# A matmul in two levels of fast products: GpSimd's additions tied to VectorE's order, and a new order of the work

## The chip, the cores and the metric

The kernel runs on one core of one Trainium2 chip. The metric is the device time of one execution in microseconds; before the change it is 1467.53 us, the median of three executions (1467.13, 1467.53 and 1470.08).

## The reference

```python
def setup_inputs():
    B, S, D = 8, 2048, 2048
    return {
        "x": np.random.randn(B, S, D).astype(np.float32),
        "w": np.random.randn(D, D).astype(np.float32),
    }

def reference(x, w):
    cs = np.cumsum(x, axis=1)
    diff = cs - np.concatenate([np.zeros((cs.shape[0], 1, cs.shape[2]), dtype=np.float32), cs[:, :-1, :]], axis=1)
    return np.matmul(diff, w).astype(np.float32)
```

The difference of a running sum is the input again, so what is computed is the product x w of a 16384 x 2048 and a 2048 x 2048 matrix.

## The kernel before

The 16384 rows are 128 tiles of 128 rows. The first 4 are multiplied plainly, since the blocks of w arrive meanwhile. The other 124 go in 31 **groups** (periods 0 to 30 in the code) of four tiles g, h, k and l. All matmuls are f16 with sums in f32, 128 x 128 by 128 x 512; four of them on one part of the contraction are a **quarter**.

A group computes a 2 x 2 block scheme of fast multiplication (tiles g, h against k, l, and the two halves of the columns), with additions in place of multiplications. Six of its products, P1, P2, P5, P3, P4 and P7, are themselves split once more into seven quarters (class `Seven`, L452; P1.0 to P1.6 on TensorE); the seventh, P6, is done whole for g and for h (P6g.0.0 and so on, L527). That makes 50 quarters, or 200 matmuls, in a group.

The names that the text uses, for a product such as P5:

- P5.s1 to P5.s4 (L463): VectorE additions of 128 x 512 f16 pieces of x, the left inputs of quarters 1, 2, 4 and 5.
- in5.Q1 (and Q4; L385): a VectorE addition of 128 x 2048 f16 pieces of w, the right input of quarter 1, made into the one buffer `flow` that all products share, so each waits until the quarter that last read it is done.
- P5.first, P5.out2 and P5.out4: ScalarE copies of the sum so far from one PSUM bank to another or to SBUF (`lent`); P5.middle: a VectorE addition that takes P5.out2 into another bank.
- S1g, S1h, S2h, S4g: VectorE additions of whole halves of tiles, 128 x 1024 f16, the inputs of the outer scheme.
- keep C11g.0, C11h+P2.0, C12g.1, C21h+P7.1: the results of the outer scheme in SBUF, f32, copied by ScalarE or added from PSUM by VectorE, 128 x 512 each.
- Twelve additions of two f32 128 x 512 pieces in SBUF are GpSimd's in each group: P2.last, P3.last, P7.last and P4.last (a `lent` copy onto a result), and C12g+C21, C12h+C21, C22g+C21 and C22h+C21, two each.

x arrives as f32 in three stages of a buffer F (`load`, L129, on SyncE's queue), is cast to f16 by ScalarE in place (`narrow`, L144), checked for its range by ScalarE (`weigh`, L148), and transposed by DMA into the tiles of x (`turn`, L160, on the same queue), which gives the stage back. turn7.0 fills half of the group's eighth tile (tiles 4 to 7 of a group's numbers are those of the next group). Results go out from the same queue (`put`, L506).

The plain part ends with copies out.1.3.1 and the like (half, tile, piece) of PSUM banks by ScalarE; their banks are those that P1 and P2 of group 0 use. ScalarE's casts narrow2.0 and narrow3.1 belong there too: they are for group 0's tiles.

What sets the order: every operation is first recorded with a label and its engine (`record`, L98), and at the end `emit` (L104) sorts all of them by the number that a table gives the label, plus 100000 for each period. Tables stand there for periods 0, 1, 2, 28, 29 and 30, and one (`None`) for the 25 steady groups, periods 3 to 27. `after` (L86) chains each operation to the one before it on its own engine, so each engine issues in the order of the numbers. Between engines only data decides: an operation waits for what it reads, and for those that still use what it writes.

Of the kernel before, what the change touches and what calls it, by code (L numbers as in the profile page):

```python
# [10 lines left out]
def kernel(  # L11
# [41 lines left out]
    B11, T1, B12, T2, B21, T3s, B22, T4 = (  # L53
        [fours[:, k, i // 2, i % 2] for k in range(KH)] for i in range(8)
    )
# [48 lines left out]
    def emit(places):  # L104
        def when(op):
            at, label = op[:2]
            own = places[at] if at in places else places[None]
            return at * PERIOD + own[label]

        for _, _, engine, ask in sorted(ops, key=when) if places else ops:  # L110
            after(engine, ask)
        ops.clear()

# [575 lines left out]
    def judge():  # L689
# [42 lines left out]
            'numbers': -648116, 'first x.1.0': -635524, 'first x.2.3': -593898,  # L732
            'first x.0.1': -583215, 'first x.0.3': -573021, 'cast w.0.1': -565802,
            'first x.0.2': -513040, 'first x.1.1': -509724, 'numbers turned': -509328,
# [517 lines left out]
```

## Time and profile before

| | |
|---|---|
| median of three executions | 1467.53 us |
| the profiled execution | 1465.45 us, of which the span is 1463.4 |
| TensorE busy | 1426.9 us, 97% of the span |
| VectorE, ScalarE, GpSimd busy | 1319.0, 1050.7, 531.5 us |
| GpSimd's additions | 372, mean 1445 ns |
| granted clock of TensorE, mean | 0.997 |

TensorE's busy time is the floor for this order of matmuls, so the question at each place is what TensorE waits for. VectorE is busy for 90% of the span and feeds TensorE, ScalarE and GpSimd; GpSimd is idle for two thirds of it. A line of the timeline gives the start, the time, the engine, the line of the code, the operation, out<-in, the count and, in brackets, the idle time before it and what ended that. The additions that `tensor` records are all on L116, copies and casts L119, quarters L440 and L533. Group 0 starts at about 72 us, group 3 at 213.5 and group 28 at 1317.5.

### The profile page before, as it was taken

How to read it: one execution, taken by the hardware profiler on the slowest of the kernel's cores; microseconds unless marked ns; L12 is line 12 of the kernel's file. 1: busy time of each engine (PE TensorE's matmuls, PEld its weight loads, DVE VectorE, ACT ScalarE, POOL GpSimd, SP SyncE). 2: the span in 40 equal slices, each digit the busy share in tenths (PEclk: the TensorE clock that was granted, in tenths of full speed). 3: DMA queues.
4: the chain of work that ended last, by engine and by line, in shares of the span. 5: the costliest groups of instructions: out<-in, count | busy, mean ns of one | idle time of the engine just before them, and what ended most of it. 6: DMA issues, size and time to landing. Idle time of an engine off the chain costs nothing. (4 is left out here: it accounts for less than half of the span.)

```text
span 1463.4 us, 20495 instructions
## 1 busy us (share of the span) xinstructions
PE 1426.9 (97%) x6543; PEld 631.4 (43%) x6543; DVE 1319.0 (90%) x2107; ACT 1050.7 (72%) x1716; POOL 531.5 (36%) x376
## 2 busy tenths in 40 slices
PE   8989999999999999999999999999999999999997
PEld 4434344444444444444444444444444444444443
DVE  2889889999999989999999999999999999999998
ACT  5877867777777777777777777777777677777663
POOL 0004432344433344423344423344423444423444
PEclk9999999999999999999999999999999999999999
DMA  9998778888787898888888888888788888888873
GB/s 365 345 245 225 202 222 240 250 230 237 231 255 234 239 232 241 231 238 248 244 236 241 231 240 249 252 228 246 223 251 248 240 235 233 224 251 239 259 213 120
DMA packets 343790, 351.62 MB, mean 240 GB/s; under 512 B 270976, under 2 KB 270976, under 8 KB 343680
## 3 DMA queue, kind: packets, MB, share of 16 engines
q1 hardware_dynamic: 343680, 350.29, 84.1%
q8 instruction: 52, 0.85, 0.2%
q14 instruction: 58, 0.48, 0.1%
HBM read 150.99 MB, written 134.22 MB: 195 GB/s over the span
## 5 line engine op out<-in xcount | busy, mean ns | idle before, releaser
L116 POOL TENSOR_TENSOR arena<-arena 128x512 f32<-128x512 f32 x372 | 531.3, 1445 | 926.7 <-DVE arena L116 728.2
L119 ACT COPY arena<-b 128x512 f32<-128x512 f32 x729 | 411.5, 590 | 267.9 <-PE b L440 197.0
L440 PE MATMUL b<-W,x 128*128 128x512 f16 x2108 | 526.6, 380 | 0.9 <-ACT b L119 0.4
L440 PEld LDWEIGHTS <-x 128*128 128x128 f16 x3224 | 313.0, 98 | 399.1 <-issue 20.8
L116 DVE TENSOR_TENSOR arena<-W 128x2048 f16<-128x2048 f16 (+1 forms) x287 | 359.9, 1255 | 45.0 <-PE b L440 44.6
L440 PE MATMUL b<-W,arena 128*128 128x512 f16 x1364 | 340.2, 379 | 9.4 <-ACT b L119 6.9
L440 PEld LDWEIGHTS <-arena 128*128 128x128 f16 x1984 | 192.5, 98 | 254.5 <-DVE arena L116 22.1
L440 PE MATMUL b<-arena,x 128*128 128x512 f16 x1116 | 286.0, 380 | 6.7 <-ACT arena L119 6.3
L119 ACT CAST F<-F 128x1024 f16<-128x1024 f32 x248 | 257.2, 1050 | 41.4 <-DMA F<-in_x_dram 40.5
L116 DVE TENSOR_TENSOR arena<-arena,b 128x512 f32<-128x512 f32 x372 | 250.9, 679 | 14.8 <-PE b L440 9.6
L153 ACT ACTIVATE F<-F 128x1024 f16<-128x1024 f16 x248 | 263.1, 1061 | 1.1
L533 PE MATMUL b<-W,x 128*128 128x512 f16 x992 | 240.5, 379 | 4.1 <-DVE x L116 2.9
L116 DVE TENSOR_TENSOR x<-x,x 128x1024 f16<-128x1024 f16 (+1 forms) x372 | 222.9, 607 | 12.2 <-PE b L440 3.3
L119 ACT COPY b<-b 128x512 f32<-128x512 f32 x186 | 107.8, 580 | 76.3 <-DVE arena L116 56.2
L440 PE MATMUL b<-arena 128*128 128x512 f16 x620 | 159.1, 379 | 2.6 <-DVE arena L116 2.2
L116 DVE TENSOR_TENSOR b<-b,arena 128x512 f32<-128x512 f32 x217 | 150.2, 693 | 8.8 <-ACT arena L119 7.6
L533 PEld LDWEIGHTS <-x 128*128 128x128 f16 x992 | 94.7, 98 | 128.3 <-DVE x L116 17.8
L116 DVE TENSOR_TENSOR arena<-b,arena 128x512 f32<-128x512 f32 x155 | 106.1, 685 | 20.4 <-PE b L440 20.2
L116 DVE TENSOR_TENSOR arena<-x 128x512 f16<-128x512 f16 x124 | 73.3, 591 | 0.1
L116 DVE TENSOR_TENSOR arena<-x,x 128x512 f16<-128x512 f16 x124 | 62.4, 503 | 3.7 <-PE b L440 1.4
L116 DVE TENSOR_TENSOR x<-x 128x512 f16<-128x512 f16 x124 | 64.4, 519 | 0.9
L254 PE MATMUL b<-W,arena 128*128 128x512 f16 x240 | 54.8, 379 | 2.6 <-ACT W L119 2.4
(43 smaller groups left out, 304.0 us busy)
## 6 DMA issues: line engine op xcount, KB each, us to landing
F<-in_x_dram SPq DMA_DIRECT2D x248, 512.0 KB, 5.1
out_dram<-arena SPq DMA_DIRECT2D x240, 512.0 KB, 5.4
W<-in_w_dram SPq DMA_DIRECT2D x32, 512.0 KB, 9.5
out_dram<-arena SPq DMA_DIRECT2D x32, 256.0 KB, 3.2
W<-in_x_dram SPq DMA_DIRECT2D x16, 256.0 KB, 6.5
x<-F SPq DMA_TRANSPOSE x248, 3.3
```

Source lines behind the costliest of these rows:

```text
L116: record(label, engine, lambda: on.tensor_tensor(dst, p, q, op))
L119: record(label, "act", lambda: nc.scalar.copy(to, p))
L153: return nc.scalar.activation(other, data, ABS, accum_out=m)
L254: said = nc.tensor.matmul(to[n], xP[:, r, ko, :], b[:, n, :], start=(ko == 0), stop=(ko == KO - 1))
L440: said = nc.tensor.matmul(to, a[:, ds(k * P, P)], b[:, k, :], start=(start and k == 0), stop=(k == 3), skip_group_check=True,)
L533: said = nc.tensor.matmul(to[n], half(t, 0)[:, k, :], T2[k][:, n, :], start=False, stop=(k == KH - 1), skip_group_check=True,)
```

## The change

`emit` now ties each GpSimd addition to the VectorE operation that was emitted last before it: the addition waits until that operation is done, whether or not it reads its result. And all seven tables are replaced. No operation is added, removed or given to another engine.

```diff
         for _, _, engine, ask in sorted(ops, key=when) if places else ops:
             after(engine, ask)
+            if engine == "pool" and "dve" in last:
+                in_turn(last["pool"], last["dve"])
         ops.clear()
+
+    def in_turn(later, first):
+        tc.add_manual_dep(
+            later.ins,
+            first.ins.name,
+            mybir.DependencyInfo(mybir.DependencyClass.Sync, mybir.DependencyReason.DATA),
+            reason="GpSimd after VectorE, in the order of places",
+        )
...
         None: {
...
-            'S2h': 13382, 'P6g.1.1': 13785, 'P5.s1': 13929, 'P2.4': 14251, 'P2.out4': 14372,
-            'P2.last': 15346, 'P2.5': 15487, 'C11g+P2.1': 15743, 'P2.6': 15807,
...
+            'C11h+P2.0': 18274, 'P6h.0.0': 20162, 'in5.Q1': 20364, 'P5.first': 20601,
+            'P2.last': 21182, 'P5.s2': 21300, 'load5.0': 23180, 'load4.0': 24591,
```

The lines of the code after the helper stand 10 lower than before (L116 is now L126, L119 is L129).

**VectorE in a steady group, around P2.last.** Rows give line, operation, out<-in with the buffers' numbers, and the shape. Before, from C11h+P2.1 to in5.Q1: C11h+P2.1, S1h, S2h, P5.s1, C11g+P2.1, C11h+P2.0, P5.s2, in5.Q1.

```order
L116 TENSOR_TENSOR arena_70<-arena_70,b7_81 128x512
L116 TENSOR_TENSOR x30_68<-x30_68,x31_69 128x1024
L116 TENSOR_TENSOR x10_64<-x30_68,x10_64 128x1024
L116 TENSOR_TENSOR arena_70<-x30_68 128x512
L116 TENSOR_TENSOR arena_70<-arena_70,b5_79 128x512
L116 TENSOR_TENSOR arena_70<-arena_70,b6_80 128x512
L116 TENSOR_TENSOR arena_70<-arena_70,x20_66 128x512
L116 TENSOR_TENSOR arena_70<-W_58 128x2048
```

And in the changed kernel, from S1h on: S1h, P5.s1, S2h, C11h+P2.0, in5.Q1, P5.s2, C11g+P2.1, S4g.

```order
L126 TENSOR_TENSOR x30_68<-x30_68,x31_69 128x1024
L126 TENSOR_TENSOR arena_70<-x30_68 128x512
L126 TENSOR_TENSOR x10_64<-x30_68,x10_64 128x1024
L126 TENSOR_TENSOR arena_70<-arena_70,b6_80 128x512
L126 TENSOR_TENSOR arena_70<-W_58 128x2048
L126 TENSOR_TENSOR arena_70<-arena_70,x20_66 128x512
L126 TENSOR_TENSOR arena_70<-arena_70,b5_79 128x512
L126 TENSOR_TENSOR x01_63<-x01_63,x00_62 128x1024
```

GpSimd's P2.last had its number behind P5.s1 and waited only for C11h+P2.1 and ScalarE's P2.out4; now it has its number behind in5.Q1 and waits for that too. C11h+P2.1 has moved up, C11g+P2.1 down behind P5.s2.

**VectorE at the seam of two steady groups.** Before, from C21g+P7.1: C21g+P7.1, P4.middle, C21h+P7.1, P4.s4, C21g+P4.0, in1.Q1 (of the next group), C21h+P7.0, P1.s2, C21g+P4.1, P1.s3.

```order
L116 TENSOR_TENSOR arena_70<-arena_70,b3_77 128x512
L116 TENSOR_TENSOR b7_81<-b5_79,arena_70 128x512
L116 TENSOR_TENSOR arena_70<-arena_70,b1_75 128x512
L116 TENSOR_TENSOR x21_67<-x21_67 128x512
L116 TENSOR_TENSOR arena_70<-arena_70,b6_80 128x512
L116 TENSOR_TENSOR arena_70<-W_58 128x2048
L116 TENSOR_TENSOR arena_70<-arena_70,b0_74 128x512
L116 TENSOR_TENSOR arena_70<-arena_70,x00_62 128x512
L116 TENSOR_TENSOR arena_70<-arena_70,b7_81 128x512
L116 TENSOR_TENSOR arena_70<-x00_62,x10_64 128x512
```

And in the changed kernel, from P4.middle: P4.middle, P4.s4, C21g+P4.0, C21h+P7.0, P1.s2, C21h+P7.1, in1.Q1, C21h+P4.0, C21g+P4.1, P1.s4, P1.s3.

```order
L126 TENSOR_TENSOR b7_81<-b5_79,arena_70 128x512
L126 TENSOR_TENSOR x21_67<-x21_67 128x512
L126 TENSOR_TENSOR arena_70<-arena_70,b6_80 128x512
L126 TENSOR_TENSOR arena_70<-arena_70,b0_74 128x512
L126 TENSOR_TENSOR arena_70<-arena_70,x00_62 128x512
L126 TENSOR_TENSOR arena_70<-arena_70,b1_75 128x512
L126 TENSOR_TENSOR arena_70<-W_58 128x2048
L126 TENSOR_TENSOR arena_70<-arena_70,b4_78 128x512
L126 TENSOR_TENSOR arena_70<-arena_70,b7_81 128x512
L126 TENSOR_TENSOR arena_70<-x00_62,arena_70 128x512
L126 TENSOR_TENSOR arena_70<-x00_62,x10_64 128x512
```

in1.Q1 has moved behind C21h+P7.0 and C21h+P7.1; C22h+C21.0 waits for C21h+P7.0, P7.last for C21h+P7.1 just ahead of in1.Q1, and C22h+C21.1 for P1.s4. On TensorE, P1.1, which needs in1.Q1, is now the fourth quarter of P1 to be issued (P1.0, P1.2, P1.3, P1.1) and P1.0 has moved up among the last quarters of the group before.

**ScalarE in the head, from the last copies of the plain part on.** Before: out.1.0.1, P1.out2, the two casts narrow2.0 and narrow3.1, P1.out4, out.1.3.0, out.1.3.1, out.1.2.0, P2.first.

```order
L119 COPY arena_70<-b1_75 128x512
L119 COPY arena_70<-b2_76 128x512
L119 CAST F_61<-F_61 128x1024 x2
L119 COPY arena_70<-b2_76 128x512
L119 COPY arena_70<-b6_80 128x512
L119 COPY arena_70<-b7_81 128x512
L119 COPY arena_70<-b4_78 128x512
L119 COPY b4_78<-b6_80 128x512
```

And in the changed kernel: out.1.2.1, P1.out2, out.1.2.0, out.1.3.0, P1.out4, narrow2.0, P2.first, out.1.3.1, narrow3.1.

```order
L129 COPY arena_70<-b5_79 128x512
L129 COPY arena_70<-b2_76 128x512
L129 COPY arena_70<-b4_78 128x512
L129 COPY arena_70<-b6_80 128x512
L129 COPY arena_70<-b2_76 128x512
L129 CAST F_61<-F_61 128x1024
L129 COPY b4_78<-b6_80 128x512
L129 COPY arena_70<-b7_81 128x512
L129 CAST F_61<-F_61 128x1024
```

P1.out4 and three copies of the plain part have moved ahead of the casts.

More of the change, by code (lines that the diff above doesn't have):

```diff
@@ L724 @@
         0: {
[7 rows of a table removed]
-            'numbers': -648116, 'first x.1.0': -635524, 'first x.2.3': -593898,
-            'first x.0.1': -583215, 'first x.0.3': -573021, 'cast w.0.1': -565802,
-            'first x.0.2': -513040, 'first x.1.1': -509724, 'numbers turned': -509328,
[157 rows of a table removed]
-        },
[47 rows of a table removed]
-        },
[46 rows of a table removed]
[7 rows of a table added]
+            'first x.0.0': -710913, 'cast w.0.0': -708588, 'numbers turned': -640017,
+            'eye': -620640, 'first x.0.1': -615478, 'first x.2.3': -611089,
[156 rows of a table added]
+        },
[47 rows of a table added]
+        },
[46 rows of a table added]
         },
         28: {
[44 rows of a table removed]
[44 rows of a table added]
         },
         29: {
[44 rows of a table removed]
[45 rows of a table added]
         },
         30: {
[42 rows of a table removed]
[43 rows of a table added]
         },
         None: {
[45 rows of a table removed]
[44 rows of a table added]
         },
```

856 rows, old and new, of the table places are left out of this document.

## The prediction

> **What bounds the kernel now.** I read the page first, then the busy time by stage, then what each engine waits for, then single groups of the timeline.
>
> ```profile
> span 1463.4 us, 20495 instructions
> PE 1426.9 (97%) x6543; PEld 631.4 (43%) x6543; DVE 1319.0 (90%) x2107; ACT 1050.7 (72%) x1716; POOL 531.5 (36%) x376
> L116 POOL TENSOR_TENSOR arena<-arena 128x512 f32<-128x512 f32 x372 | 531.3, 1445 | 926.7 <-DVE arena L116 728.2
> L116 DVE TENSOR_TENSOR arena<-x 128x512 f16<-128x512 f16 x124 | 73.3, 591 | 0.1
> ```
>
> TensorE is the bound at 97%; GpSimd has slack and waits mostly for VectorE already. The last row matters: VectorE's small f16 additions take 591 ns on average. By stage (start:end, length, then busy time of PE, PEld, DVE, ACT, POOL, clock, DMA share, GB/s), and for one good and one bad group:
>
> ```profile
> 0.00:213.50 213.50, 198.31 (x919) 87.42 (x919) 163.01 (x268) 157.47 (x239) 41.21 (x33) 0.98 0.89 269
> 213.50:1317.50 1104.00, 1093.45 (x5013) 485.02 (x5012) 1022.88 (x1631) 804.40 (x1330) 428.06 (x303) 1.00 0.85 239
> 1317.50:1463.40 145.90, 135.09 (x614) 58.94 (x612) 133.14 (x210) 88.83 (x148) 62.20 (x42) 0.99 0.72 207
> 350.40:393.92 43.52, 43.52 (x201) 19.41 (x200) 40.43 (x66) 32.12 (x53) 17.00 (x13) 1.00 0.87 249
> 525.85:571.00 45.15, 43.98 (x202) 19.32 (x201) 41.13 (x66) 32.08 (x53) 16.66 (x13) 1.00 0.89 234
> ```
>
> The second row is the 25 steady groups: 1104.00 / 25 = 44.16 us each. The fourth is one in which nothing goes wrong: 43.52. The fifth is group 10, which lost 1.6 us. So between a steady group and a clean one lie 25 x (44.16 - 43.52) = 16.0 us. The end of the chain of waits gives the floor:
>
> ```profile
> 1430.52 6.05 PE b L440 x28
> ...
> 1451.84 1.40 POOL arena L116
> ...
> 1458.48 0.69 DVE arena L116
> ```
>
> 28 matmuls in 6.05 us are 0.216 each; a quarter (4) is 0.865 and a group (200) 43.2. A clean group is thus within 0.32 us of the floor.
>
> The same place in a clean group (9) and in group 10, from the timeline:
>
> ```profile
> 500.53 1.56 POOL L116 TENSOR_TENSOR arena<-arena 128x512 f32<-128x512 f32 x1 [4.30 <-ACT arena L119]
> 500.54 0.42 DVE L116 TENSOR_TENSOR arena<-x 128x512 f16<-128x512 f16 x1
> 502.60 1.22 DVE L116 TENSOR_TENSOR arena<-W 128x2048 f16<-128x2048 f16 x1
> 503.12 1.03 PE L440 MATMUL b<-W,arena 128*128 128x512 f16 x4
> ```
>
> ```profile
> 543.69 1.42 DVE L116 TENSOR_TENSOR x<-x,x 128x1024 f16<-128x1024 f16 x2
> 544.90 1.34 POOL L116 TENSOR_TENSOR arena<-arena 128x512 f32<-128x512 f32 x1 [4.30 <-ACT arena L119]
> 545.03 1.50 DVE L116 TENSOR_TENSOR arena<-x 128x512 f16<-128x512 f16 x1
> 547.75 0.57 ACT L119 COPY b<-b 128x512 f32<-128x512 f32 x1 [1.88 <-DVE arena L116]
> 548.37 1.02 PE L440 MATMUL b<-W,arena 128*128 128x512 f16 x4 [0.72 <-ACT b L119]
> ```
>
> In both, GpSimd's P2.last and VectorE's P5.s1 meet. In group 9 they start 0.01 us apart, P5.s1 takes 0.42 and P2.last 1.56. In group 10, P5.s1 comes 0.13 later and takes 1.50, nearly until GpSimd is done, and the lost microsecond passes through the copy P5.first and P5.s2 to TensorE, which pauses. Whoever is first keeps the other out. P2.last is set free by ScalarE at a fixed place in the group; P5.s1 stands behind S1h and S2h (the row at 543.69), which wait for transposes:
>
> ```profile
> POOL arena L116 <- DVE arena L116: 728.2, 90, 94.4
> DVE x L116 <- DMA x<-F: 2.9, 6, 0.8
> PEld L440 <- DVE arena L116: 23.2, 54, 1.4
> ```
>
> The second row is that wait: 6 times, at most 0.8 us, enough to lose 0.01 or 0.13. The third is what TensorE's weight loads then wait for VectorE.
>
> By the Trainium skill ("SBUF — State Buffer", section "Who interferes with whom") a VectorE operation with two SBUF inputs contends with a GpSimd instruction that reads SBUF, and "Issue order, not op shape, decides who blocks". The 0.42 against 1.50 and the 1.34 against 1.56 agree.
>
> **The change, part by part.** *Steady groups.* The added wait costs no instruction. Nine of the twelve GpSimd additions of a group already wait, through their data, for the VectorE operation ahead of them or one as late; it binds at three: P2.last (behind in5.Q1), C22g+C21.0 (behind in7.Q1), C22h+C21.1 (behind P1.s4). The first is the cure: P5.s1, S2h and in5.Q1 all stand ahead of P2.last now, so none of them can lose to it, however late the transposes land.
>
> What waits for P2.last then? Counted from the start of P2.6 on TensorE: a quarter's result is out after 1.03 (row at 503.12), C11h+P2.0 and in5.Q1 take 0.69 and 1.22, GpSimd 1.34 to 1.56, so P2.last ends at 4.3 to 4.5. Its buffer is next written by P5.out2, after P5.2, four quarters on: 4 x 0.865 + 1.03 = 4.5. P5.out2 is a copy of 0.57 (row at 547.75), and P5.4, which needs it, starts at 7 x 0.865 = 6.06. About 0.9 us is left: the later P2.last is covered by P5.1 and P6h.1.0. If P5.1 were late, that cover would grow, not go.
>
> At C22g+C21.0 only C21g+P4.0 and put2 wait behind, many quarters later. At C22h+C21.1 the train of additions ends; behind it are a store and, on VectorE, in1.Q4, which may wait some tenths while TensorE has P2.0, P1.4 and P1.5 to do. These two I cost at nothing.
>
> The gain is bounded by 0 (the pauses come back elsewhere) and 16.0 (every group clean). The order on all engines is new, so new joints are tight: in1.Q1 to P1.4, and P7.s3 to P7.5, have some 0.1 us by the durations above. I take 12, that is a group of 44.16 - 0.48 = 43.68, since the nearest row, the clean group, has the same pitch of work and its joints cost 0.32 in all; half as much again is allowed for the new ones.
>
> *Head.* The timeline, with two stretches of 20 us:
>
> ```profile
> 78.92 1.04 ACT L119 CAST F<-F 128x1024 f16<-128x1024 f32 x1 [2.63 <-DMA F<-in_x_dram]
> 81.95 1.04 ACT L119 CAST F<-F 128x1024 f16<-128x1024 f32 x1 [1.98 <-DMA F<-in_x_dram]
> 82.90 2.27 ACT L119 COPY arena<-b 128x512 f32<-128x512 f32 x4
> 83.53 1.87 PE L440 MATMUL b<-arena,x 128*128 128x512 f16 x4 [4.31 <-ACT arena L119]
> 85.20 3.62 PE L440 MATMUL b<-W,x 128*128 128x512 f16 x8
> 60.00:80.00 20.00, 18.29 (x84) 8.09 (x83) 19.80 (x31) 13.47 (x22) 0.00 (x0) 1.00 1.04 233
> 80.00:100.00 20.00, 16.47 (x63) 6.79 (x63) 12.99 (x21) 14.24 (x26) 1.59 (x1) 0.83 1.01 282
> ```
>
> ScalarE stands in two casts whose loads are late, with P1.out4 behind them, and TensorE waits 4.31 us. It then runs at half pace: 4 matmuls in 1.87 and 8 in 3.62, 0.43 each against 0.216, on a granted clock of 0.83 in that stretch. Twelve matmuls lose 12 x 0.21 = 2.5 us. The change puts P1.out4 ahead of both casts. At most 4.3 + 2.5 = 6.8 us go; at least none, since the DMA engines are full here (share 1.04 and 1.01), the loads come no sooner, and the next to wait are out.1.3.1, which now stands behind one cast and frees the bank of P2.1, and S1h behind turn3.0. I take 4: the 4.31, less a fraction of a wait like the 1.98 of the second cast, with some of the half pace left.
>
> The Trainium skill ("TensorE: Matmul & The Clock Gate", Part 1) has the clock halve after an idle window of some 3.4 us. The 4.31 and the 0.83 agree; by that rule a pause of the 1.98 kind would not halve the clock, and the head would gain up to 5.
>
> *Groups 1, 2, 28 to 30 and the end.* In the last stage 145.90 - 135.09 = 10.8 us are not TensorE's; most is the tail after its last quarter. P4.last now stands behind C21h+P4.0 and VectorE's last addition after GpSimd's as before. I bound this at +-2, by one GpSimd addition (1.40 in the chain) and one of VectorE (0.69) more or less on the tail, and take 0.
>
> *Sum.* The profiled execution took 1465.45, 2.05 around its span and 2.1 below the median 1467.53. 1465.45 - 12 - 4 = 1449.5; I say 1450.
>
> **The rivals.** *The change doesn't do what it says for the time:* the pauses come back at another meeting of VectorE and GpSimd. For it: all six kinds of GpSimd meeting stay, and 90% of VectorE's time is taken. Against: the added wait fixes who is first at each. The steady groups then gain 1 or 2, the head 4: 1462.
>
> *Tight joints:* six joints with 0.1 us or less slip by 0.1 in each group: 25 x 0.6 = 15 us, the gain of the steady groups gone: 1465.
>
> *Slower: GpSimd takes the ports ahead of in1.Q1.* The seam of two groups before:
>
> ```profile
> 521.33 11.74 POOL L116 TENSOR_TENSOR arena<-arena 128x512 f32<-128x512 f32 x8 [4.59 <-DVE arena L116]
> 523.24 0.93 DVE L116 TENSOR_TENSOR arena<-x 128x512 f16<-128x512 f16 x1
> 527.77 1.26 DVE L116 TENSOR_TENSOR arena<-W 128x2048 f16<-128x2048 f16 x1 [0.36 <-PE b L440]
> ```
>
> GpSimd runs a train here, 11.74 / 8 = 1.47 each. In1.Q1 waits for TensorE (P4.6); P7.last follows inside the train and stands ahead of in1.Q1 in the new order, so nothing but time decides. Adding durations, P7.last starts 0.04 us behind in1.Q1, less than the spread of one addition (1.34 to 1.56). If P7.last is first by 0.1 or more, in1.Q1 waits some 1.13 (1.50 - 0.42 is 1.08 in the row of group 10). P1.1 comes three quarters after P4.6: 2.6 - 1.03 - 1.26 leaves 0.2 to 0.3. So 0.89 a group, 22 us: 1449.5 + 22 = 1472. For it: the 0.04. Against: the row at 523.24, an f16 addition that waited only 0.5 inside the train, got in between two additions.
>
> By the same rule of the Trainium skill this rival is decided by issue order alone.
>
> **How the numbers follow.** A measurement of this kernel can tell about 0.2%, 2.9 us. Forecast (1442 to 1457): 0.50. Pauses elsewhere, 1462: 0.12. Tight joints, 1465: 0.08, half of it within 0.2%. GpSimd ahead of in1.Q1, 1472: 0.18. Slower by something in the order that I have not seen, 1471 to 1480: 0.12. So faster 0.50 + 0.12 + 0.04 = 0.66, same 0.04, slower 0.30. The range runs from 1441 (16 for the steady groups, 6.8 for the head, 1.5 for the end: 1465.45 - 24.3) to 1474, over the seam's 1472, leaving out 0.1 above and below. The forecast's own range is 1442 to 1457.
>
> **What would show it.** Right: the 25 steady groups in 1087 to 1094 us; the 128x512 arena<-x additions well below 591 ns; no copy P5.first that waits 1.88 for VectorE; in the head no cast between P1.out2 and P1.out4, and no 4.31 ahead of a matmul. Wrong: an arena<-W 128x2048 row far above 1.26 at the seam, with TensorE idle behind it in nearly every group; idle time of GpSimd behind VectorE that ends in a ScalarE copy's wait for GpSimd; or a new wait for loads in the head.

## The result

The changed kernel takes 1457.21 us, the median of six executions (1455.76 to 1460.77), against 1466.22 (six executions beside it, 1462.83 to 1470.08). The ratio is 0.9941, with a 95% interval from 0.9922 to 0.9960: faster, by half of what was forecast (1450 from 1467.53). The profiled execution took 1456.21 us, 9.24 less than the one before.

The page of the changed kernel:

```profile
span 1454.3 us, 20618 instructions
PE 1424.5 (98%) x6543; PEld 630.1 (43%) x6543; DVE 1302.5 (90%) x2107; ACT 1046.1 (72%) x1716; POOL 552.1 (38%) x376
L126 POOL TENSOR_TENSOR arena<-arena 128x512 f32<-128x512 f32 x372 | 551.9, 1491 | 896.8 <-DVE arena L126 623.7
L126 DVE TENSOR_TENSOR arena<-x 128x512 f16<-128x512 f16 x124 | 59.3, 479 | 1.2 <-PE b L450 0.2
```

VectorE's small additions fell from 591 to 479 ns, and GpSimd's grew from 1445 to 1491. In the 25 steady groups 50 of GpSimd's additions take over 1.8 us, against 26 before: it gives way more often. VectorE still loses some meetings, at other places: S4g takes 1.16 in every steady group where it took 0.69 before (the row of group 12 below), and in1.Q4 1.69 in 24 of them where it took 1.22.

```profile
633.19 1.16 DVE L126 TENSOR_TENSOR x<-x,x 128x1024 f16<-128x1024 f16 x1
```

No quarter is late for it: the pauses ahead of P1.6, which reads in1.Q4, and ahead of P3's quarters, which need S4g, come to 0.1 us in the 25 groups. The 25 steady groups, and one of them, in the changed kernel (busy time by stretch, columns as before):

```profile
214.65:1305.05 1090.40, 1089.48 (x5001) 483.13 (x5000) 1003.39 (x1625) 797.93 (x1326) 445.60 (x301) 1.00 0.85 241
392.00:435.57 43.57, 43.41 (x201) 19.19 (x199) 39.84 (x65) 31.84 (x53) 17.51 (x13) 1.00 0.87 241
```

Both kernels run the same 6543 matmuls, so the fairest comparison by stage is the time at which TensorE starts the n-th one, whatever it is called. These stretches end there, first for the kernel before, then for the changed one (400, 946, 5946 and all but the last matmul, give or take one; third number: TensorE's busy time and count). The last matmul of group 2 is the 946th in both kernels, and the 5000 behind it are 25 groups' worth.

```profile
0.00:94.47 94.47, 83.46 (x400) 37.60 (x401) 54.85 (x99) 66.25 (x86) 0.20 (x4) 0.96 1.01 329
0.00:219.92 219.92, 204.54 (x947) 90.15 (x948) 169.43 (x276) 160.92 (x244) 47.41 (x37) 0.98 0.88 268
0.00:1320.97 1320.97, 1295.23 (x5946) 574.00 (x5947) 1189.35 (x1901) 965.09 (x1573) 472.74 (x337) 1.00 0.86 244
0.00:1455.90 1455.90, 1426.47 (x6542) 631.38 (x6543) 1317.52 (x2105) 1050.70 (x1716) 528.92 (x374) 1.00 0.85 241
```

```profile
0.00:88.82 88.82, 80.64 (x400) 36.73 (x401) 54.47 (x99) 65.34 (x84) 0.25 (x5) 1.00 1.03 341
0.00:221.69 221.69, 203.49 (x946) 89.49 (x947) 171.00 (x277) 163.17 (x248) 46.49 (x37) 0.99 0.89 268
0.00:1311.97 1311.97, 1292.85 (x5946) 572.60 (x5947) 1174.69 (x1902) 960.98 (x1574) 491.69 (x337) 1.00 0.86 246
0.00:1446.73 1446.73, 1424.07 (x6542) 630.09 (x6543) 1301.11 (x2106) 1046.08 (x1716) 549.73 (x375) 1.00 0.85 242
```

At matmul 400 (the end of the head) the changed kernel leads by 94.47 - 88.82 = 5.65 us. At matmul 946 it lags by 1.77. At matmul 5946 it leads by 9.00, at the end by 9.17. So the head gained 5.7, what follows up to the end of group 2 lost 7.4 (1.0 of it in the last quarters of group 0, up to matmul 546), the steady groups gained 10.8, and the end gained 0.2. These leads come from one execution of each kernel and are good to about 1 us (e9 below shows how far two executions of the same order can differ).

The 7.4 us have two visible pauses. In group 1, VectorE's P1.s4 meets GpSimd's train and stands ahead of P1.middle and P1.s3; TensorE's P1.4 waits for P1.s3. In group 2, ScalarE stands at the cast narrow6.0, whose load lands only at 183.54, with the copy keep C11h.0 and P2.out4 behind it; TensorE's P2.6 waits. From the changed kernel's timelines of VectorE, ScalarE and TensorE, put together:

```profile
124.89 1.52 DVE L126 TENSOR_TENSOR arena<-x,arena 128x512 f16<-128x512 f16 x1
127.53 0.41 DVE L126 TENSOR_TENSOR arena<-x,x 128x512 f16<-128x512 f16 x1
128.00 1.90 PE L450 MATMUL b<-W,arena 128*128 128x512 f16 x8 [1.90 <-DVE arena L126]
...
183.61 1.04 ACT L129 CAST F<-F 128x1024 f16<-128x1024 f32 x1 [2.90 <-issue]
184.82 1.07 ACT L129 COPY arena<-b 128x512 f32<-128x512 f32 x2 [0.16 <-DMA out_dram<-arena]
185.94 1.02 PE L450 MATMUL b<-arena,x 128*128 128x512 f16 x4 [2.34 <-ACT arena L129]
187.37 2.12 PE L543 MATMUL b<-W,x 128*128 128x512 f16 x5 [0.40 <-DVE x L126]
```

The second looks like what the change took out of the head, a cast ahead of an out4. That it is something else shows in e9.

### The profile page after: what moved, and what is told of

Its sections match the earlier page's. It is cut to its first block, busy times and chain, and to the rows that moved or that the text cites. A ratio compares the mean times of both kernels' runs of the same rounds, so it can differ in the third digit from the quotient of the medians.

```text
span 1454.3 us, 20618 instructions
## 1 busy us (share of the span) xinstructions
PE 1424.5 (98%) x6543; PEld 630.1 (43%) x6543; DVE 1302.5 (90%) x2107; ACT 1046.1 (72%) x1716; POOL 552.1 (38%) x376
## 5 line engine op out<-in xcount | busy, mean ns | idle before, releaser
L126 POOL TENSOR_TENSOR arena<-arena 128x512 f32<-128x512 f32 x372 | 551.9, 1491 | 896.8 <-DVE arena L126 623.7
L129 ACT COPY arena<-b 128x512 f32<-128x512 f32 x729 | 407.2, 588 | 257.6 <-PE b L450 127.7
L126 DVE TENSOR_TENSOR arena<-W 128x2048 f16<-128x2048 f16 (+1 forms) x287 | 367.6, 1281 | 23.5 <-PE b L450 23.4
L450 PE MATMUL b<-W,arena 128*128 128x512 f16 x1364 | 344.0, 379 | 5.8 <-DVE arena L126 3.8
L129 ACT CAST F<-F 128x1024 f16<-128x1024 f32 x248 | 260.2, 1049 | 44.5 <-DMA F<-in_x_dram 40.6
L450 PE MATMUL b<-arena,x 128*128 128x512 f16 x1116 | 281.6, 379 | 4.4 <-ACT arena L129 4.4
L126 DVE TENSOR_TENSOR arena<-arena,b 128x512 f32<-128x512 f32 x372 | 247.7, 678 | 11.1 <-PE b L450 9.6
L126 DVE TENSOR_TENSOR x<-x,x 128x1024 f16<-128x1024 f16 (+1 forms) x372 | 232.8, 633 | 6.2 <-DMA x<-F 3.8
L129 ACT COPY b<-b 128x512 f32<-128x512 f32 x186 | 107.3, 577 | 78.0 <-DVE arena L126 62.0
L126 DVE TENSOR_TENSOR b<-b,arena 128x512 f32<-128x512 f32 x217 | 150.1, 692 | 11.4 <-ACT arena L129 11.0
L126 DVE TENSOR_TENSOR arena<-b,arena 128x512 f32<-128x512 f32 x155 | 105.3, 681 | 18.5 <-PE b L450 17.0
L126 DVE TENSOR_TENSOR arena<-x,x 128x512 f16<-128x512 f16 x124 | 56.8, 458 | 31.9 <-PE b L450 31.7
L126 DVE TENSOR_TENSOR arena<-x 128x512 f16<-128x512 f16 x124 | 59.3, 479 | 1.2 <-PE b L450 0.2
L126 DVE TENSOR_TENSOR x<-x 128x512 f16<-128x512 f16 x124 | 56.6, 457 | 3.3 <-PE b L450 1.5
L126 DVE TENSOR_TENSOR arena<-arena,x 128x512 f16<-128x512 f16 x124 | 54.2, 437 | 2.6
```

Of the source, the lines that this page charges most:

```text
L126: record(label, engine, lambda: on.tensor_tensor(dst, p, q, op))
L129: record(label, "act", lambda: nc.scalar.copy(to, p))
L450: said = nc.tensor.matmul(to, a[:, ds(k * P, P)], b[:, k, :], start=(start and k == 0), stop=(k == 3), skip_group_check=True,)
```

## The experiments

The table gives every run's lead of TensorE over the profiled execution of the kernel before, in us, at the start of the n-th matmul, and its time against the kernel before run beside it (e5 is the median of two executions, e10 of three). Differences of less than about 1 us between two leads say nothing. All edits are numbers of the tables or the added wait.

| run | 400 | 500 | 900 | 1000 | 5900 | last | median, us | ratio (95%) |
|---|---|---|---|---|---|---|---|---|
| the change | 5.6 | 5.8 | -2.6 | -1.6 | 9.0 | 9.2 | 1457.21 | 0.9941 (0.9922 to 0.9960) |
| e1 new order, no wait | 6.2 | 6.0 | -3.8 | -3.9 | -38.1 | -44.2 | 1505.04 | 1.0260 (1.0243 to 1.0278) |
| e2 old order, wait | 0.9 | -0.7 | -7.4 | -12.5 | -187.7 | -207.5 | 1673.92 | 1.1413 (1.1389 to 1.1437) |
| e3 old order, casts later | -4.8 | -4.7 | -4.7 | -4.7 | -5.1 | -5.1 | 1471.41 | 1.0032 (1.0022 to 1.0042) |
| e4 places of groups 1, 2 | 5.6 | 5.6 | 0.1 | 1.1 | 11.5 | 11.8 | 1454.67 | 0.9922 (0.9905 to 0.9939) |
| e5 wait at P2.last only | 5.6 | 5.5 | -4.4 | -4.5 | -12.7 | -14.9 | 1482.00 | 1.0101 (1.0060 to 1.0141) |
| e6 only P1.out4 first | 2.5 | 2.6 | 2.7 | 2.7 | 0.7 | 0.8 | 1466.12 | 0.9997 (0.9982 to 1.0011) |
| e7 groups 1, 2 again | 5.5 | 5.6 | 0.1 | 1.1 | 12.1 | 11.2 | 1454.40 | 0.9914 (0.9884 to 0.9945) |
| e8 and the steady table | 5.7 | 5.6 | 0.0 | 1.1 | -2.4 | -2.9 | 1468.25 | 1.0008 (0.9996 to 1.0020) |
| e9 cast later | 6.0 | 6.0 | -1.5 | -0.5 | 9.1 | 7.9 | 1457.76 | 0.9947 (0.9927 to 0.9968) |
| e10 load earlier | 5.5 | 5.7 | -0.1 | 0.9 | 10.7 | 11.3 | 1456.21 | 0.9927 (0.9902 to 0.9953) |
| e11 sums later | 5.2 | 5.3 | -0.2 | 0.9 | 15.2 | 14.6 | 1448.40 | 0.9878 (0.9857 to 0.9899) |

Below, "the pause ahead of P1.4" is by how much TensorE starts that quarter later than the quarter before it would allow, summed over the 25 steady groups.

**e1, the new order without the wait.**

```diff
             after(engine, ask)
-            if engine == "pool" and "dve" in last:
-                in_turn(last["pool"], last["dve"])
```

> The changed kernel without the added wait; its order is kept. Theory 1 (the wait is what cures the steady groups): P2.last may again start before P5.s1 and S2h, the 25 steady groups lose 3 to 8 us of the 11.6 they gained (matmul 1000 to 5900), 1460 to 1465 us in all. Rival 1 (the new order of the engines alone makes the gain): within 1.5 us of the changed kernel, 1456 to 1459. The first two groups and their pauses stay in both.

Measured: 1505.04 us, 48 more than the changed kernel, far over what either theory allowed. The pauses ahead of P1.4 sum to some 25 us, ahead of P6h.0.0 to 15 and ahead of P5.3 to 9, in every one of the 25 groups; in the changed kernel those are 0.2, under 0.1 and 1.6. VectorE and GpSimd at the seam of two steady groups, first of the changed kernel, then of e1, whose lines stand 2 lower (GpSimd's row of e1 is a train of four, whose fourth addition is C22h+C21.1):

```profile
617.87 0.42 DVE L126 TENSOR_TENSOR arena<-x,arena 128x512 f16<-128x512 f16 x1
618.21 0.42 DVE L126 TENSOR_TENSOR arena<-x,x 128x512 f16<-128x512 f16 x1
618.43 1.32 POOL L126 TENSOR_TENSOR arena<-arena 128x512 f32<-128x512 f32 x1 [0.54 <-DVE arena L126]
```

```profile
634.98 0.42 DVE L124 TENSOR_TENSOR arena<-x,arena 128x512 f16<-128x512 f16 x1
635.31 1.49 DVE L124 TENSOR_TENSOR arena<-x,x 128x512 f16<-128x512 f16 x1
629.77 6.75 POOL L124 TENSOR_TENSOR arena<-arena 128x512 f32<-128x512 f32 x4
636.86 1.47 PE L448 MATMUL b<-W,arena 128*128 128x512 f16 x6 [0.81 <-DVE arena L124]
```

Held back by 0.54 us, C22h+C21.1 comes behind P1.s4 and P1.s3; free, it starts between the two, P1.s3 takes 1.49 instead of 0.42, and P1.4 is a microsecond late. The meeting that the prediction spoke of is there too, but with S1h, not P5.s1, as its victim (the first row is GpSimd's P2.last):

```profile
646.37 1.49 POOL L124 TENSOR_TENSOR arena<-arena 128x512 f32<-128x512 f32 x1 [2.79 <-ACT arena L127]
646.65 1.76 DVE L124 TENSOR_TENSOR x<-x,x 128x1024 f16<-128x1024 f16 x1
648.45 0.43 DVE L124 TENSOR_TENSOR arena<-x 128x512 f16<-128x512 f16 x1
```

S1h takes 1.76 instead of 0.68, P5.s1 behind it is as short as ever. The wait is what makes this order work.

**e2, the old order with the wait.**

```diff
             after(engine, ask)
+            if engine == "pool" and "dve" in last:
+                in_turn(last["pool"], last["dve"])
...
```

The helper `in_turn` that is left out here is that of the change.

> The kernel before with the added wait and its own order. There P2.last's number stands right behind P5.s1, so the wait alone takes away the meeting of the two. Theory 1: the pauses ahead of P5.2 (7.2 us in 8 of 25 groups) and the two large ones ahead of P6h go, the regular ones stay; 1457 to 1461 us. Rival 1: the wait without the order gains nothing or makes GpSimd's trains late; 1464 to 1470.

Measured: 1673.92 us, 14% slower; theory 1 falls, and rival 1 was far too mild. Of the chief waits of this run, and of the timeline of group 12 on GpSimd, ScalarE and TensorE:

```profile
PE b L450 <- ACT arena L129: 80.5, 56, 4.2
PE b L450 <- ACT b L129: 69.9, 78, 2.9
```

```profile
736.71 3.89 POOL L126 TENSOR_TENSOR arena<-arena 128x512 f32<-128x512 f32 x3 [6.24 <-DVE arena L126]
739.29 1.07 ACT L129 COPY arena<-b 128x512 f32<-128x512 f32 x2 [3.17 <-POOL arena L126]
739.93 1.02 PE L450 MATMUL b<-arena,x 128*128 128x512 f16 x4 [2.00 <-ACT arena L129]
```

GpSimd starts its train late, behind a VectorE operation; the train holds the lent buffer (P3.last), ScalarE's P4.out2 waits 3.17 us for it, and TensorE's P4.4 waits 2.00 for that. This comes back in every group (some 53 us in 25 groups ahead of P4.4). Some 50 us more come ahead of P4.2, and the rest ahead of other quarters; those were not followed up. So the wait alone costs 207 us, the order alone 38 (1505.04 against 1467.09), and the two together gain 9.

**e5, the wait at P2.last only.**

```diff
-        for _, _, engine, ask in sorted(ops, key=when) if places else ops:
+        for _, label, engine, ask in sorted(ops, key=when) if places else ops:
             after(engine, ask)
-            if engine == "pool" and "dve" in last:
+            if engine == "pool" and label == "P2.last":
```

> The changed kernel with the added wait at P2.last alone, eleven of the twelve GpSimd additions of a group free. Theory 1a (each of the binding waits guards its own place): without any added wait the steady groups lost 25.4 us ahead of P1.4, 14.9 ahead of P6h.0.0 and 9.3 ahead of P5.3; here the first stays and the other two go to what the changed kernel has, so 1480 to 1484 us. Theory 1b (the prediction's: P2.last is the place that matters): within 3 us of the changed kernel, 1457 to 1460.

Measured: 1482.00 us; the pause ahead of P1.4 is some 25 us, ahead of P5.3 0.4, ahead of P6h.0.0 nothing. TensorE's wait for VectorE's sums in `arena`, in this run and in the changed kernel:

```profile
PE b L450 <- DVE arena L126: 30.7, 38, 2.7
```

```profile
PE b L450 <- DVE arena L126: 5.9, 9, 1.9
```

Theory 1a holds: of the 48 us that the wait is worth in this order, P2.last's is 23 (1505.04 - 1482.00), and the other 25 are the waits at the remaining additions, in the trace C22h+C21.1's at the seam.

**e3 and e6, the head's casts in the old order.** In e3 both casts go behind P1.out4 and the copies of the plain part; in e6 only behind P1.out4.

```diff
+    places[0].update({'narrow2.0': -18700, 'turn2.0': -18690, 'load3.0': -18680, 'narrow3.1': -17700})
```

> The kernel before with narrow2.0 and narrow3.1 of the head moved behind P1.out4 and the copies of the plain part, and nothing else. Theory 2 (what the head gains is given back, since the chain of loads, casts and transposes of groups 1 and 2 runs at its own pace): TensorE is 4 to 6 us earlier at matmul 400 and at most 1.5 us at matmul 1000; 1464 to 1466 us in all. Rival 2 (it was given back only by the new tables of groups 1 and 2): 4 us or more are left at matmul 1000, 1460 to 1463.

```diff
+    places[0].update({'narrow2.0': -22080, 'turn2.0': -22070, 'narrow3.1': -22060})
```

> The kernel before with the casts narrow2.0 and narrow3.1 of the head (and the transpose turn2.0) placed right behind P1.out4; the copies of the plain part stay behind the casts. The prediction's head step: the 4.3 us ahead of P1.6 and the half clock go, matmul 400 is 4 us or more earlier. Rival 2a (the wait only moves: out.1.3.0 behind the casts holds P2.0, the loads come no sooner): 0 to 2.5 us at matmul 400, 1464 to 1467 us in all.

Neither expectation on e3 was right: it loses 4.8 us by matmul 400. TensorE and ScalarE of e3 (the last row is ScalarE's out.1.3.0), then TensorE and ScalarE of e6:

```profile
82.96 1.89 PE L440 MATMUL b<-W,x 128*128 128x512 f16 x8 [2.77 <-ACT arena L119]
...
93.94 1.87 PE L533 MATMUL b<-W,x 128*128 128x512 f16 x4 [4.71 <-ACT arena L119]
82.32 0.59 ACT L119 COPY arena<-b 128x512 f32<-128x512 f32 x1 [3.23 <-DMA out_dram<-arena]
```

```profile
78.84 1.03 PE L440 MATMUL b<-arena,x 128*128 128x512 f16 x4
82.70 3.44 PE L440 MATMUL b<-W,x 128*128 128x512 f16 x8 [2.84 <-ACT arena L119]
```

```profile
78.18 0.58 ACT L119 COPY arena<-b 128x512 f32<-128x512 f32 x1 [2.11 <-PE b L440]
78.66 1.05 ACT L119 CAST F<-F 128x1024 f16<-128x1024 f32 x1
81.12 1.04 ACT L119 CAST F<-F 128x1024 f16<-128x1024 f32 x1 [1.41 <-DMA F<-in_x_dram]
82.08 0.58 ACT L119 COPY arena<-b 128x512 f32<-128x512 f32 x1
```

In e6 P1.6 runs on time (78.84 instead of 83.53), and 2.84 us come ahead of P2.0 instead, whose bank the copy out.1.3.0 frees (82.08). 2.5 us are left, as its rival 2a had it. The copy stands behind the casts there, but without them it would hardly come sooner: in e3 it stands ahead of them and still starts at 82.32, after 3.23 us of waiting for a store. The store is put out.0.3.0, which reads the buffer that out.1.3.0 writes; it lands at 82.30 in e3 and at 81.89 in e6. In e3 the casts stand behind the copies that wait so, and load3.0, which follows turn2.0, is issued at 87.26 instead of 81.97, with all that hangs on it late.

The changed kernel's table issues that store at 62.41, where the old table issued it at 76.06; it lands at 66.83, and its copies can run ahead of the casts. load3.0 is issued at 79.98. That the rest of the 5.7 us comes from the earlier stores and load is read from the traces; no run moved them alone. The gain is the table's and not the wait's: e1, with the new tables and no wait, leads by 6.2 at matmul 400, and e2, with the wait and the old tables, by 0.9.

What settles theory 2: e6's 2.5 us at matmul 400 are 2.7 at matmul 1000. Nothing in the loads of groups 1 and 2 takes a lead of that size back in the old tables. Theory 2 (the loads' own pace) falls, and what was lost behind the head was lost to the new tables; e7 and e10 below agree. (Its 2.7 shrink to 0.8 later, where the old steady table paused ahead of P5.2 and P6h.0.0 13 times, against 10 in the kernel before; the time, 1466.12, isn't told apart from the kernel before.)

**e4, e7, e9, e10: places in groups 1 and 2.** narrow6.0 and turn6.0 behind P2.out4 (A); load6.1 ahead of put1.1 and of the range check see.5, which writes into the same stage (B); P1.middle and P1.s3 ahead of P1.s4 (C). e9 is A alone, e10 is B alone, e7 all three (its numbers are set out by part below). In e4 two numbers of C were counted from the wrong period, so P1.middle and P1.s3 of group 1 were made far too late, P1.4 and what follows used older sums, and the product came out wrong. Its row stands in the table, but nothing is built on it.

```diff
+    places[1].update({'narrow6.0': 104300, 'turn6.0': 104350,                    # A
+                      'see.5': 77800, 'put1.1': 69700,                           # B
+                      'P1.out2': -22900, 'P1.middle': -22850, 'P1.s3': -22800})  # C
```

> The changed kernel with six numbers of group 1's table changed: narrow6.0 and turn6.0 behind P2.out4 of group 2; load6.1 no longer behind put1.1 and the range check see.5; P1.middle and P1.s3 ahead of P1.s4. Theory 2 as it stands (the loads' own pace): at most 1 us at matmul 1000, 1456 to 1458 us. Rival 2 (places in the tables hold the chain of loads and TensorE back): the pauses ahead of P1.4 in group 1 (2.1) and P2.6 in group 2 (2.5) shrink and 3 to 5 us are left at matmul 1000; 1452 to 1454.

> The changed kernel with seven numbers of group 1's table changed: narrow6.0 and turn6.0 behind P2.out4 of group 2; load6.1 no longer behind put1.1 and the range check see.5; in group 1 P1.out2, P1.middle and P1.s3 ahead of P1.s4. Theory 2 (the pace of the loads): at most 1 us of the changed kernel's lag at matmul 1000 comes back; 1456 to 1458 us. Rival 2 (places): the pause ahead of P1.4 in group 1 goes, that ahead of P2.6 in group 2 halves; 2.5 to 4.5 us come back at matmul 1000, 1452.5 to 1455.

> The changed kernel with only narrow6.0 and turn6.0 of group 1 behind P2.out4 of group 2. If the cast ahead of P2.out4 is what holds P2.6 (2.5 us): half of the pause or more goes, 1 to 2.5 us come back at matmul 900. If S1h's late transposes (turn7.0) hold the same place by themselves: under 0.7 us, the pause moves to P6h.0.0.

> The changed kernel with only load6.1 of group 1 freed of put1.1 and the range check see.5. If this chain of load, cast and transpose is what holds group 2: load7.0 and turn7.0 come 1.5 to 2.5 us sooner, S1h too, and 1 to 2.5 us come back at matmul 900. If the cast narrow6.0 ahead of P2.out4 holds it by itself: under 0.7 us.

At matmul 1000 e7 leads by 1.1 where the changed kernel lags by 1.6: 2.7 us back, as the rival had it, and the pause ahead of P1.4 in group 1 fell from 2.1 to 0.5. The whole times of e7, e9 and e10 are not told apart from the changed kernel's: their intervals overlap with its own. P2.6 of group 2, in e10 and in e9:

```profile
184.37 1.02 PE L450 MATMUL b<-arena,x 128*128 128x512 f16 x4 [0.56 <-ACT arena L129]
```

```profile
184.93 1.02 PE L450 MATMUL b<-arena,x 128*128 128x512 f16 x4 [2.00 <-ACT arena L129]
```

B alone does nearly all: load6.1 is issued at 161.81 instead of 165.98, and 2.5 us are back at matmul 900. load6.0, put2.1 and turn7.0 behind it are issued within 0.2 us of where they were, yet each lands 1.6 us sooner, and S1h, which waits for turn7.0, runs 1.6 us sooner too. A alone seems to bring 1.1, but 1.0 of that is there at matmul 746, at 169 us, before the moved cast has its turn at 184.76: it is the difference between two executions of the same order, and A brings nothing that can be told from none.

With the cast out of the way, ScalarE in e9 stands at keep C11h.0, the copy ahead of P2.out4:

```profile
183.80 1.07 ACT L129 COPY arena<-b 128x512 f32<-128x512 f32 x2 [3.81 <-DMA out_dram<-arena]
```

It waits for put2.1 of group 1, a store that still reads the buffer it writes. In the changed kernel that store lands at 184.79 and the copy starts at 184.82; in e9, e10 and e7 the two are 183.78 and 183.80, 183.22 and 183.24, 182.13 and 182.15. So in none of these traces was it the cast that held P2.6. The new table issues put2.1 at 177.45, behind load6.0; the old one issued it at 169.56, and it landed at 173.66. The late links are thus on SyncE's queue: the load, held by a store and a range check that both wait for GpSimd's additions, and the store put2.1. Moving put2.1 was not tried. The other 4.7 us of the 7.4 are spread over pauses of 0.4 to 1.6 us (ahead of P7.5, P1.4, P2.6, P5.0 and others); which places cause each was not tried.

**e8 and e11, the steady pauses that were left.** The changed kernel still pauses ahead of P2.4 (3.1 us) and P4.1 (3.4) in every group. Both runs carry e7's numbers.

```diff
+    places[None].update({'P2.s4': 8300, 'P7.2': 56905, 'P4.0': 60500})   # e8
+    places[None].update({'P2.s4': 8300, 'C11h+P2.1': 26000})             # e11
```

> The same seven numbers and three of the steady table: P2.s4 behind P2.s3, P7.2 ahead of P4.1, P4.0 ahead of P7.1. If the two regular pauses left in the changed kernel (ahead of P2.4, 3.1 us in 25 groups, and ahead of P4.1, 3.4 us) come from these rows: 5 to 6.5 us below the kernel with the seven numbers alone, 1447 to 1450. If they only move to the next tight joint: within 2 us of it.

> The changed kernel with the seven numbers of group 1 and two of the steady table: P2.s4 behind P2.s3, and the addition C11h+P2.1 moved from ahead of in2.Q4 to behind S4g (it is then made after P2.last; the sum is the same). With P2.s4 moved, the 3.1 us ahead of P2.4 went, and 4.2 us more came ahead of P5.3, whose copy waits for VectorE's run from P2.s3 to C11h+P2.0. If that run is what P5.3 waits for, taking one addition (0.60 us) out of it lets both go: 3 to 5 us below the seven numbers alone, 1449.5 to 1452. If another joint takes it over: 1453 to 1456.

In e8 both pauses went, but 19.1 us came ahead of P7.5 and 5.7 ahead of P5.3, and it lost what the change had gained, far outside both expectations. TensorE's wait for a VectorE sum in PSUM was 0.6 us in all in the changed kernel and is in e8

```profile
PE b L450 <- DVE b L126: 15.7, 27, 0.6
```

e11 keeps only the move of P2.s4 and takes C11h+P2.1 out of VectorE's run ahead of P5.3. The pause ahead of P2.4 went, that ahead of P5.3 fell to 0.4, that ahead of P4.1 to 1.6, and the steady groups lead by 14.3 us more at matmul 5900 than at 1000 (10.6 in the changed kernel). Its page begins, for its profiled execution of 1450.40 us:

```profile
span 1448.5 us, 20596 instructions
```

At 1448.40 us (ratio 0.9878, 0.9857 to 0.9899), a little under the 1449.5 to 1452 expected, it beats both kernels.

## Why the prediction was right or wrong

- **Direction and range: right.** 1457.21 lies between 1441 and 1474, just outside the forecast's own 1442 to 1457, and the change is faster; the gain is 9 us where 17.5 were forecast. Part of that is luck: a term that was put at nothing cost 7.4 us, and the range, drawn for other reasons, was wide enough to hold it.
- **Steady groups, -12: right in size.** 10.8 us between matmuls 946 and 5946, and 1090.40 us for the 25 groups, inside the 1087 to 1094 named. The rows that the term started from were a little unfair: the stretch before holds 13 matmuls more than 25 groups (x5013), so 2.8 us of its 16.0 were work, and the clean group's 43.52 holds 201, so its joints cost 0.1 and not 0.32.
- **The cure at P2.last: right, but half of it.** The pauses that it was to take away, ahead of P5.2 and P6h.0.0, sum to 9.8 us before and to nothing now; no P5.s1, S1h or S2h of the 25 groups meets GpSimd. "These two I cost at nothing" was true of the cost of the wait at C22h+C21.1 (in1.Q4 behind it waits the "some tenths" that were named, 0.47 us), but not of its worth: e1 and e5 show 25 us there, as much as the 23 at P2.last. The text asked who waits for the delayed addition and not who would have lost the ports to it.
- **Head, -4: right in kind.** 5.7 us by matmul 400; the upper bound of 6.8 holds. The reason was too narrow: e6 did only what the text costed and gained 2.5. The text looked for the next wait among casts and transposes; what came next was a copy that waits for a store, and the new table issues that store 14 us sooner.
- **The step that failed: "Groups 1, 2, 28 to 30 and the end. I bound this at +-2 ... and take 0."** The bound was taken from the tail alone, where it held (0.2 us). Groups 0, 1 and 2 have tables of their own, and those were not worked through behind the head: 7.4 us were lost there. Between the two profiled executions the sum forecast 16 and 9.2 came: the head gave 1.7 more, the steady groups 1.2 less, and these groups account for the rest. The prediction had named one of the faults elsewhere, an f16 addition in GpSimd's train, and it stood in group 1's table; the other, a store placed too late, it had not named.
- **The rivals.** "GpSimd takes the ports ahead of in1.Q1" did not come true in the changed kernel: in 24 of 25 groups P7.last starts 0.07 to 0.09 us behind in1.Q1 (the estimate was 0.04); in1.Q1 takes 1.22 or 1.23 in those and 1.69 in the other, and P7.last gives way with 2.25 to 2.28. But its mechanism and its price are right. In group 7 of e10, and in group 7 of e11 as well, the two start within 0.01 us and GpSimd is first: in1.Q1 takes 2.34 and 2.35, P7.last 1.26, and P1.1 comes 0.87 and 0.88 late, where the prediction said 0.89. VectorE's in1.Q1 and TensorE's P1.1 of e10:

```profile
438.34 2.34 DVE L126 TENSOR_TENSOR arena<-W 128x2048 f16<-128x2048 f16 x1 [0.49 <-PE b L450]
440.74 1.02 PE L450 MATMUL b<-arena 128*128 128x512 f16 x4 [0.71 <-DVE arena L126]
```

  In group 7 of e7 they start equally close, and in1.Q1 keeps its 1.23. So the order hangs on 0.08 us, and that it held in every group of the changed kernel is in part luck. The tight joints cost what the forecast allowed: 9.8 us of pauses in 25 groups, 0.39 each over the floor of 43.2, where 0.48 were taken.

## What to carry to other kernels

When an order and a wait are changed together, price them together: here each alone was a loss (38 and 207 us) and the pair a gain, since the wait says who is first at each meeting and the order decides what that costs. Work through the short tables at the start with the same care as the steady one, and compare stages by the n-th matmul, not by a label that the new order has moved. Where a wait delays an operation, ask also which neighbour it saves. Where a copy is late, look for the store that still reads its buffer before blaming what stands ahead of it: both in the head and in group 2 the cast hid one.

## What was not expected of the hardware

The meetings are settled with a resolution of less than a tenth of a microsecond. An f16 addition of VectorE that starts 0.07 to 0.09 us ahead of GpSimd keeps its time (in1.Q1 1.22, GpSimd's addition 2.28 instead of 1.32), and one that comes 0.23 us behind waits it out (P1.s3 1.49). Within 0.01 us either can be first: in1.Q1 was in e7 (1.23), and was not in e10 and e11 (2.34, 2.35). VectorE's sums from PSUM go on at 0.60 a piece through GpSimd's trains all the while (C21h+P4.0 and C21g+P4.1 start at 616.68 and 617.27, under a P7.last that runs from 615.61 to 617.89). The Trainium skill ("SBUF — State Buffer", section "Who interferes with whom") has both: a VectorE instruction with at most one SBUF input, outside the two-port modes, does not contend, and with two the first to issue blocks the other. The traces agree.

TensorE's half pace did not follow the length of the pause alone. After 2.77 us (e3) eight matmuls took 1.89, full pace, at a granted clock of 1.00; after 2.84 (e6) eight took 3.44, half, and the clock was 0.58 from 82.5 to 86.5 us; in the changed kernel, 2.34 and then 0.40 us, four matmuls apart, were followed by five in 2.12, half again, and the clock was 0.70 from 186 to 190. The Trainium skill ("TensorE: Matmul & The Clock Gate", Part 1) speaks of an idle window of some 3.4 us. The pauses here are shorter, so the prediction's sentence that a pause of about 2 us would leave the clock alone is no rule to rely on, though e9's 2.00 us did.
